# Norms in steps between products at four seams of two fused blocks, other banks for the outward products, other engines for the splits

## The chip, the cores and the metric

One core of a Trainium2 chip runs the whole program. The metric is the device time of one execution in microseconds (us); lower is better. A kernel's time is the median of its runs, and one further execution was taken by the profiler.

## What is computed

Two transformer blocks one after the other on x of 1024 tokens by 1024 features, all in float32. The first: attention over a chosen subset of keys, then a gated FFN with a short convolution (width 2816), both under adaptive norms. The second: a sliding-window attention beside a linear recurrence, then an FFN of width 4096. Cut to what the change touches:

```python
# first block
x = x + gt_m * dsa_mixer(rmsnorm(x, g_mix) * (1 + sc_m) + sh_m)
h = rmsnorm(x, g_ffn) * (1 + sc_f) + sh_f
x = rmsnorm(x + gt_f * conv_ffn(h), g_final)
# second block
u = rmsnorm(h, g_pre_mix)
mix = concat(attention(u), recurrence(u)) @ w_out
h = h + rmsnorm(mix, g_post_mix)
u = rmsnorm(h, g_pre_ffn)
f = square(relu(u @ w_ff1)) @ w_ff2
h = h + rmsnorm(f, g_post_ffn)
```

Each rmsnorm needs the sum of squares of a token over all 1024 features before any normed value of the token exists.

## The kernel before

Features lie on the 128 partitions in 8 tiles, tokens along a row in two halves (hf = 0, 1) of 512. A float32 product is made of three matmuls (`mm3`): each operand is split into a high part and a remainder (`wh` by ScalarE in `hi`, `wl` by VectorE or GpSimd in `lo`), and low by high, high by low and high by high are added in PSUM. One k-step of 128x512 is three matmuls on TensorE (PE). PSUM has eight banks; `pairs` 0 and 1 are banks 0 to 3 taken two by two, and shown as pair_70 and pair_71 in the orders and rows; banks 4 to 7 are bank_72 to bank_75. `self.psum(...)` says which banks each kind of tile takes in turn.

A norm is: squares on ScalarE, added up on VectorE or GpSimd (`square_sums`), summed over the partitions by PE against a column of ones (`token_sums`, shown as `ones,sq`), a reciprocal root of 12 operations of 128x4 on VectorE (`rstd`, rows rv, rs_t, ry), a broadcast by PE (`bcast`, shown as `ident,ry`), and a multiply per tile that reads the broadcast's bank.

PE's instructions run in the order in which the program is written (`MANUAL`). The other engines' orders are set by the framework's scheduler from its own estimate of when things are ready; each engine then runs its queue strictly in order. Buffers in SBUF are 49 equal slots (`slot`, `free`), handed out first in, first out; SyncE (SP) issues the loads and stores in order.

The four seams:
- **A.** `dsa_out` makes the output tiles of the attention and, after each half, that half's norm; `ffn_lead` then makes the first two feature tiles F0 and F1 of the FFN, half 0 before half 1, u and g each. F0 writes into pairs, F1 into banks 4 to 7. GpSimd runs `weight_sums` (adds of weights for the seven-product method, rows rt, ra, rb) and half of the splits beside it.
- **B.** `ffn1` ends with the gate of the last tiles: t is multiplied (L1358) out of a pair, and GpSimd makes s and v of a pair of tiles (L1304), which are stored. `seven_out` then runs seven products P1, P5, P2, P6, P3, P7, P4, each over 11 k-steps, whose banks `out_plan` alternates between banks 0 to 3 and 4 to 7. `make` loads and splits ahead.
- **C.** `between(hf)` is the norm after the first FFN and the one of the second block in one. Its half 1 runs over `second`, between the units of half 0 (a unit is 24 matmuls): sums after unit `UNIT_AT[0]`, broadcast after `UNIT_AT[1]`.
- **D.** `seven_lead` makes, for n = 0 to 15, a product "11" (12 matmuls) and, one n later, "12" (12 matmuls) into the same bank; between them stand the steps of `mix_norm(1)` (sums, broadcast with the combinations fa for the next stage), `mix_out(0)` and `mix_out(1)` (the sums and roots of other norms). `LEAD_AT` says after which n. `ahead` loads weights three n ahead and splits them two ahead, on GpSimd and VectorE in turn.

## Time and profile before

| | us |
|---|---|
| median of 3 runs | 2335.28 |
| lowest, highest | 2328.22, 2336.17 |
| the profiled execution, its own time | 2344.45 |
| its span, first to last instruction | 2342.7 |

| engine | busy us | share |
|---|---|---|
| PE (TensorE) | 2149.9 | 92% |
| DVE (VectorE) | 1381.5 | 59% |
| ACT (ScalarE) | 1033.8 | 44% |
| POOL (GpSimd) | 883.1 | 38% |

The mean granted clock of TensorE over the span is 0.959 of full speed. The stages lie in the span about so: attention to 592, first FFN 596 to 1098, its outward products 1105 to 1321, second block's units and attention 1321 to 1667, lead of the last FFN 1667 to 1790, the rest of it to the end. How to read it: a row of the timeline gives start, length, engine, line, operation with its output and inputs by their names, and in brackets how long the engine stood idle before and which instruction released it.

### The profile page before, as it was taken

What the parts mean: (1) busy time and instruction counts of PE and PEld (TensorE: products, weight loads), DVE (VectorE), ACT (ScalarE), POOL (GpSimd) and SP (SyncE); (2) the same over time, 40 slices, a digit from 0 to 9 for tenths busy, and PEclk for the clock granted to TensorE, in tenths of its full rate; (3) what the DMA queues carried; (4) which work ended last, traced back from release to release, by engine and by line L of the source; (5) the groups of instructions that cost most, each with busy time, mean ns of one, the idle gap of its engine ahead of it and who ended that gap; (6) DMA issues with size and microseconds to landing.
All of it is one profiled execution on the core that took longest, in us unless ns stands there. A gap on an engine that the chain in (4) does not pass through costs nothing.

```text
span 2342.7 us, 28433 instructions
## 1 busy us (share of the span) xinstructions
PE 2149.9 (92%) x10073; PEld 1785.7 (76%) x10073; DVE 1381.5 (59%) x2306; ACT 1033.8 (44%) x1623; POOL 883.1 (38%) x557
## 2 busy tenths in 40 slices
PE   5875899998799999998999899999888999999997
PEld 4664788976588888887788777788667888788886
DVE  8889686789421111122667777685673554643475
ACT  4765566643121221222443366765464443544441
POOL 6225331054366756656442422233341444201002
PEclk8977999999899999999999999999999999999999
DMA  7001131174366667686997422124255776866571
GB/s 281 1 9 52 42 99 37 46 266 165 126 202 236 240 207 236 233 275 238 323 338 279 144 69 67 55 64 154 89 211 204 261 241 221 318 195 201 191 258 54
DMA packets 165442, 405.60 MB, mean 173 GB/s; under 512 B 18441, under 2 KB 19761, under 8 KB 165298
## 3 DMA queue, kind: packets, MB, share of 16 engines
q1 hardware_dynamic: 164144, 399.58, 49.9%
q10 hardware_dynamic: 1154, 4.20, 0.5%
q8 instruction: 79, 1.29, 0.2%
q14 instruction: 65, 0.53, 0.1%
HBM read 292.28 MB, written 111.43 MB: 172 GB/s over the span
## 4 chain that ended last, share of the span: by engine, by line
PE 59%; DVE 11%; DMA 8%; POOL 4%; issue 3%; ACT 3%; SPq 0%; DVEq 0%; POOLq 0%; ACTq 0%
PE pair L208 29%; PE bank L208 27%; DVE ada L387 1%; POOL wlo L228 1%; DMA tc<-ra 1%; DMA early<-e 1%; DMA ada<-in_ada_dram 1%; POOL rt L2034 1%; DMA ra<-in_ff_dram 1%; PE bank L1134 1%; DVE sq L306 1%; DVE wl L228 1%; DMA rb<-in_ff_dram 1%; DMA st<-hs 1%; POOL rb L2034 1%
## 5 line engine op out<-in xcount | busy, mean ns | idle before, releaser
L208 PE MATMUL pair<-h,whi 128*128 128x512 f32 x1408 | 439.2, 394 | 3.2 <-DVE h L343 3.1
L228 POOL TENSOR_TENSOR wlo<-wraw,whi 128x1024 fp32r<-128x1024 f32 x98 | 245.5, 2511 | 435.1 <-ACT whi L225 310.6
L228 DVE TENSOR_TENSOR wl<-st,wh 128x1024 fp32r<-128x1024 f32 x189 | 250.3, 1341 | 207.3 <-ACT wh L225 141.0
L225 ACT ACTIVATE wh<-st 128x1024 fp32r<-128x1024 f32 x189 | 197.4, 1059 | 297.7 <-PE pair L208 67.6
L208 PEld LDWEIGHTS pair<-h,whi 128*128 128x128 f32 x1408 | 267.8, 191 | 62.2 <-DVE h L343 6.6
L208 PE MATMUL pair<-h,wlo 128*128 128x512 f32 x704 | 277.5, 396 | 28.9 <-ACT h L225 19.9
L225 ACT ACTIVATE whi<-wraw 128x1024 fp32r<-128x1024 f32 x121 | 127.1, 1056 | 313.2 <-POOL wlo L228 137.0
L343 DVE SCALAR_TENSOR_TENSOR t<-pair,vec,t 128x1023 f32<-128x1023 f32 (+1 forms) x42 | 53.8, 1282 | 261.7 <-ACT t L1350 250.0
L208 PE MATMUL pair<-wh,wl 128*128 128x512 f32 x432 | 170.4, 394 | 16.1 <-DVE t L1358 7.5
L208 PEld LDWEIGHTS pair<-h,wlo 128*128 128x128 f32 x704 | 133.8, 190 | 59.0 <-issue 23.6
L208 PE MATMUL pair<-wl,wh 128*128 128x512 f32 x432 | 169.3, 392 | 0.0
L208 PE MATMUL pair<-wh 128*128 128x512 f32 x432 | 169.1, 391 | 0.0
L208 PE MATMUL bank<-u,whi 128*128 128x512 f32 x448 | 141.7, 398 | 0.0
L2327 POOL TENSOR_TENSOR acc<-acc,grow 128x512 f32<-128x512 f32 x16 | 23.3, 1468 | 292.0 <-ACT sq L2326 292.0
L208 PE MATMUL bank<-fa,wh 128*128 128x512 f32 x416 | 130.0, 394 | 0.0
L208 PE MATMUL bank<-wh,wl 128*128 128x512 f32 x324 | 127.4, 393 | 0.0
L208 PE MATMUL bank<-wh 128*128 128x512 f32 x324 | 126.4, 390 | 0.0
L208 PE MATMUL bank<-wl,wh 128*128 128x512 f32 x324 | 126.2, 389 | 0.0
L208 PE MATMUL pair<-fa,wh 128*128 128x512 f32 x352 | 111.3, 398 | 0.0
L208 PEld LDWEIGHTS pair<-wh,wl 128*128 128x128 f32 x432 | 81.8, 189 | 36.2 <-DVE t L1358 8.0
L208 PEld LDWEIGHTS bank<-u,whi 128*128 128x128 f32 x448 | 86.6, 193 | 18.0
L208 PEld LDWEIGHTS pair<-wh 128*128 128x128 f32 x432 | 81.8, 189 | 17.2
(504 smaller groups left out, 4981.6 us busy)
## 6 DMA issues: line engine op xcount, KB each, us to landing
st<-hs SPq DMA_DIRECT2D x173, 256.0 KB, 4.2
ada<-in_ada_dram SPq DMA_DIRECT2D x48, 512.0 KB, 6.0
wraw<-in_f_in_dram SPq DMA_DIRECT2D x44, 512.0 KB, 4.1
wraw<-in_w_in_dram SPq DMA_DIRECT2D x33, 512.0 KB, 3.6
ra<-in_ff_dram SPq DMA_DIRECT2D x32, 512.0 KB, 4.5
rb<-in_ff_dram SPq DMA_DIRECT2D x32, 512.0 KB, 5.5
st<-td SPq DMA_DIRECT2D x64, 256.0 KB, 3.6
hs<-s SPq DMA_DIRECT2D x54, 256.0 KB, 3.7
```

The lines of the kernel that those rows point to most:

```text
L208: self.nc.tensor.matmul(out, w, x, start=start, stop=stop, **k)
L225: self.nc.scalar.activation(out, src, AF.Copy, **k)
L228: (eng or self.nc.vector).tensor_tensor(out, src, hi.bitcast(F32), op=ALU.subtract)
L306: (eng or nc.vector).tensor_tensor(acc, acc, sq, op=ALU.add)
L343: (eng or self.nc.vector).scalar_tensor_tensor(out, a, s, b, op0=op0, op1=op1)
L387: nc.vector.scalar_tensor_tensor(raw, raw, 1.0, self.cond, op0=ALU.mult, op1=ALU.mult, accum_out=c)
L1134: nc.tensor.transpose(ps[:, at:at + P], pr[j][:, bs(kt)], self.ident)
L2034: add = lambda o, a, b: nc.gpsimd.tensor_tensor(o, a, b, op=ALU.add)
L2327: self.nc.gpsimd.tensor_tensor(a, a, self.grow[:, hs(i)], op=ALU.mult)
```

## The change

`dsa_out` now makes the norm of half 0 alone. That of half 1 is a generator, `ffn_norm`, stepped in `ffn_lead`: squares before the first product, sums and root after u of F0, half 0, broadcast and multiply after g of F0, half 0. `ffn1` gives it banks 7 and 5.

`out_plan` takes `swap=True` for the first FFN: P1, P2, P3 and P4 go to banks 4 to 7 and P5, P6 and P7 to banks 0 to 3. The norm's banks 0 and 4 there change places.

`UNIT_AT` is (2, 3) instead of (1, 2), and `between(1)` squares tiles 4 to 7 before 0 to 3.

`LEAD_AT` now names an n and a place (0 after its "11", 1 after the "12" that follows): the steps stand at (2, 0), (2, 1), (3, 1), (6, 1), (14, 0). The first four weights of the lead are split on GpSimd, all others on VectorE. The products' banks go round as 4, 5, 6, 7, 2, 0 instead of 0, 2, 4, 5, 6, 7. The stores in `mix_out` stand before its root.

```diff
@@ -72,8 +72,9 @@
 WSTART = 4
 VLATE = 2
 MIX_AT = (1, 3, 7)
-LEAD_AT = (0, 1, 2, 12, 14)
-UNIT_AT = (1, 2)
+LEAD_AT = ((2, 0), (2, 1), (3, 1), (6, 1), (14, 0))
+LEAD_BY_POOL = 4
+UNIT_AT = (2, 3)
 SUM_BY = lambda nc: (None, nc.gpsimd)
 REST2 = 2
 UNITS2 = ((4, 5, 0, 1, 6, 7, 8, 9, 2, 3, "scan", 10, 11, 12, 13), (6, 7, 8, 9, 4, 5, "scan", 0, 1, 2, 3, 10, 11, 12, 13))
@@ -1276,21 +1277,32 @@
                     self.free(*self.oT.values())
             self.free(*self.po[hf])
             self.mod_steps(len(self.steps) - KT)
-            r = self.rstd(self.sumsq([x1[m][:, hs(hf)] for m in range(KT)]), D)
-            packs[hf] = self.norm_mod(x1, hf, r, self.gsf, 3)
+            if hf == 0:
+                r = self.rstd(self.sumsq([a[:, hs(0)] for a in x1]), D)
+                packs[0] = self.norm_mod(x1, 0, r, self.gsf, 3)
         self.hp = packs
 
+    def ffn_norm(self):
+
+        acc = self.square_sums([a[:, hs(1)] for a in self.x1])[0]
+        yield
+        r = self.rstd(self.token_sums(acc), D)
+        yield
+        self.hp[1] = self.norm_mod(self.x1, 1, r, self.gsf, 3)
+
 
     def ffn1(self):
 
         nc = self.nc
-        self.psum(main=[4, 5, 6, 7], MAIN=[0, 1], U=[0, 1], fo=[4, 5, 6, 7])
+        self.psum(main=[4, 5, 6, 7], MAIN=[0, 1], U=[0, 1], fo=[4, 5, 6, 7], ssq=[7], rb=[5])
         self.rot["G"] = self.rot["U"]
         self.ahead = (4, 2)
         st = nc.sync.dma_start
         sums = self.chain(self.weight_sums(*self.t_out1), self.weight_sums(*self.t_in2), self.weight_sums(*self.t_out2))
         lo, hi = slice(0, HF), slice(HF, S)
-        lead = self.ffn_lead()
+        norm = self.ffn_norm()
+        next(norm)
+        lead = self.ffn_lead(norm)
         t = {}
         for n, f in enumerate(FFN1):
             t[n % 2] = lead[n] if n < 2 else self.ffn_in(f)
@@ -1311,7 +1323,7 @@
             self.free(a, b, s, v)
             if n == NF1 - 3:
                 self.out_plan(NF1 // 2, self.I["f_out"], self.t_out1[1], AHEAD_OUT1,
-                              [lambda k, i=i: self.hs1[k][i] for i in (0, 3, 1, 4, 6, 5, 2)])
+                              [lambda k, i=i: self.hs1[k][i] for i in (0, 3, 1, 4, 6, 5, 2)], True)
                 self.make(0)
         self.free(*self.hp[0], *self.hp[1])
         self.ffn1_out(sums)
@@ -1323,13 +1335,15 @@
                 self.mm3(ps[:, hs(hf)], self.terms(self.weights((kind, f)), self.hp[hf]))
         return self.ffn_gate(f, pu, pg)
 
-    def ffn_lead(self):
+    def ffn_lead(self, norm):
+
 
         pairs = self.bank2("u"), self.bank2("g")
         apart = [[self.bank("fo") for _ in range(2)] for _ in range(2)]
         for hf in range(2):
             for j, kind in enumerate("ug"):
                 self.mm3(pairs[j][:, hs(hf)], self.terms(self.weights((kind, FFN1[0])), self.hp[hf]))
+                next(norm, None)
             for j, kind in enumerate("ug"):
                 self.mm3(apart[j][hf], self.terms(self.weights((kind, FFN1[1])), self.hp[hf]))
         return [self.ffn_gate(FFN1[0], *pairs), self.ffn_gate(FFN1[1], *apart)]
@@ -1398,7 +1412,7 @@
 
         def hook(name, k):
             if (name, k) in NORM1_AT:
-                self.rot.update(ssq=deque([0]), rb=deque([4]))
+                self.rot.update(ssq=deque([4]), rb=deque([0]))
                 next(norm, None)
             if (name, k) == ("P4", 6):
                 self.ahead = AHEAD2
@@ -1424,7 +1438,9 @@
             nc.vector.tensor_tensor(self.gf2, self.vall("g_final"), self.vall("g_final"), op=ALU.mult)
             self.up, self.r1 = {}, {}
         xs = [self.x1[m][:, hs(hf)] for m in range(KT)]
-        a1, a2 = self.square_sums(xs, [self.gf2[:, m:m + 1] for m in range(KT)], SUM_BY(nc)[hf])
+
+        order = [*range(4, KT), *range(4)] if hf else range(KT)
+        a1, a2 = self.square_sums([xs[m] for m in order], [self.gf2[:, m:m + 1] for m in order], SUM_BY(nc)[hf])
         yield
         ps = self.bank("ssq")
         for i, a in enumerate((a1, a2)):
@@ -1890,6 +1906,10 @@
         xs = [self.mx[hf][m // 2][:, m % 2] for m in range(KT)]
 
         sq = self.square_sums(xs)[0]
+        for m in range(4):
+            nc.sync.dma_start(self.x3[hf, m], self.mx[hf][m])
+        if hf:
+            self.free(*self.mx[0], *self.mx[1])
         yield
         r = self.rstd(self.token_sums(sq), D)
         e = self.eps4[hf] = self.const(f"eps4_{hf}", [P, 4])
@@ -1897,10 +1917,6 @@
         nc.vector.tensor_tensor(e, e, e, op=ALU.mult)
         nc.vector.reciprocal(e, e)
         nc.vector.tensor_scalar(e, e, EPS, None, op0=ALU.mult)
-        for m in range(4):
-            nc.sync.dma_start(self.x3[hf, m], self.mx[hf][m])
-        if hf:
-            self.free(*self.mx[0], *self.mx[1])
 
     def second(self):
         self.psum(main=[4, 5, 6, 7], ga=[0], gx=[2], vT=[0], ssq=[1], rb=[3])
@@ -1936,7 +1952,7 @@
 
     def second_mix(self):
 
-        self.psum(main=[4, 5, 6, 7], f1=[0, 2, 4, 5, 6, 7], ssq=[0], rb=[1, 2, 3])
+        self.psum(main=[4, 5, 6, 7], f1=[4, 5, 6, 7, 2, 0], ssq=[0], rb=[1, 2, 3])
         self.residual(0)
         norm, out = self.mix_norm(0), self.mix_out(0)
         next(norm)
@@ -1955,9 +1971,8 @@
         norm, out = self.mix_norm(1), self.mix_out(1)
         next(norm)
         steps += [norm, norm, out, out]
-        G, V = self.nc.gpsimd, self.nc.vector
         self.seven_lead(NPAIR2, lambda n: self.I["ff1"][n], self.fa, self.relu_square, self.early,
-                        dict(zip(LEAD_AT, steps)), deque([V, G]))
+                        dict(zip(LEAD_AT, steps)))
         self.ffn2_in()
         self.ffn2_out()
 
@@ -2068,7 +2083,7 @@
         self.nc.scalar.activation(out, src, AF.Relu)
         self.nc.scalar.activation(out, out, AF.Square)
 
-    def seven_lead(self, N, src, fa, put, early, at, by):
+    def seven_lead(self, N, src, fa, put, early, at):
 
         raw, w = deque(), deque()
 
@@ -2076,8 +2091,7 @@
             while len(w) + len(raw) + got[0] < min(n + 3, N):
                 raw.append(self.load("r0", src(len(w) + len(raw) + got[0])))
             while raw and len(w) + got[0] < min(n + 2, N):
-                by.rotate(1)
-                w.append(self.split_here(raw.popleft(), by[0]))
+                w.append(self.split_here(raw.popleft(), self.nc.gpsimd if len(w) + got[0] < LEAD_BY_POOL else None))
 
         got = [0]
         before = None
@@ -2088,6 +2102,7 @@
                 got[0] += 1
                 self.prod(ps, [a[:, :HF] for a in ab], fa["11"])
                 self.nc.scalar.activation(e[:, :HF], ps, AF.Copy)
+                next(at.get((n, 0), iter(())), None)
             if before:
                 m, wb, eb, pb = before
                 self.prod(pb, [a[:, HF:] for a in wb], fa["12"], True)
@@ -2095,8 +2110,7 @@
                 self.nc.sync.dma_start(early[m], eb)
                 self.free(*wb, eb)
             before = n, ab, e, ps
-            if n in at:
-                next(at[n], None)
+            next(at.get((n, 1), iter(())), None)
         self.free(*fa.pop("11"), *fa.pop("12"))
 
     def seven_in(self, N, fa, load, split, dest, mid, end, before_last):
@@ -2145,9 +2159,11 @@
         last()
         self.free(*[a for k in fa.values() for a in k])
 
-    def out_plan(self, N, right, sums, ahead, left):
+    def out_plan(self, N, right, sums, ahead, left, swap=False):
 
         X, Y = self.banks[:4], self.banks[4:]
+        if swap:
+            X, Y = Y, X
         b = lambda i, j: lambda k: right[k + N * i][:, hs(j)]
         t = lambda i: lambda k: sums[k][i]
         self.plan2 = [(n, left[i], Y if i in (1, 3, 5) else X, n in ("P2", "P7"), r) for i, (n, r) in enumerate((
```

What this does to the orders, at three places. PE at A, before, from the end of F0's u of half 0 (`h` are the normed rows, `ident,ry` is the broadcast of half 1):

```order
L208 MATMUL pair_70<-h_5535,wlo_5779 128x512
L208 MATMUL pair_70<-h_5535,whi_5778 128x512 x2
L339 MATMUL pair_71<-ident,ry_5839 128x128 x4
L208 MATMUL pair_71<-h_5500,wlo_5906 128x512
L208 MATMUL pair_71<-h_5500,whi_5905 128x512 x2
```

And in the change, two pieces, the first at the end of F0's u, the second at the end of its g:

```order
L209 MATMUL pair_70<-h_5535,whi_5778 128x512 x2
L313 MATMUL bank_75<-ones,sq_5813 128x1 x4
L209 MATMUL pair_71<-h_5500,wlo_5843 128x512
```

```order
L209 MATMUL pair_71<-h_5530,whi_5842 128x512 x2
L209 MATMUL pair_71<-h_5535,wlo_5843 128x512
L209 MATMUL pair_71<-h_5535,whi_5842 128x512 x2
L340 MATMUL bank_73<-ident,ry_5879 128x128 x4
L209 MATMUL bank_72<-h_5500,wlo_5847 128x512
```

The sums stood before F0's u and stand behind it; the broadcast stood between u and g, in the same pair as g, and stands behind g in a bank of its own.

GpSimd (POOL) at C, before: the seven adds of the squares (`sq`) with two weight splits (`wlo`) among them, all behind the splits of half 0's normed rows (`u`):

```order
L228 TENSOR_TENSOR u_1523_10592<-nt_1517_10570,u_1523_10592 128x512
L228 TENSOR_TENSOR u_1525_10600<-nt_1516_10569,u_1525_10600 128x512
L228 TENSOR_TENSOR wlo_1562_10858<-wraw_1553_10798,whi_1561_10857 128x1024
L306 TENSOR_TENSOR sq_1542_10732<-sq_1542_10732,sq_1544_10736 128x512
L306 TENSOR_TENSOR sq_1542_10732<-sq_1542_10732,sq_1545_10740 128x512
L228 TENSOR_TENSOR wlo_1582_10984<-wraw_1575_10939,whi_1581_10983 128x1024
L306 TENSOR_TENSOR sq_1542_10732<-sq_1542_10732,sq_1546_10744 128x512
L306 TENSOR_TENSOR sq_1542_10732<-sq_1542_10732,sq_1547_10748 128x512
L306 TENSOR_TENSOR sq_1542_10732<-sq_1542_10732,sq_1548_10752 128x512
L306 TENSOR_TENSOR sq_1542_10732<-sq_1542_10732,sq_1549_10756 128x512
L306 TENSOR_TENSOR sq_1542_10732<-sq_1542_10732,sq_1550_10760 128x512
```

And in the change:

```order
L307 TENSOR_TENSOR sq_1542_10732<-sq_1542_10732,sq_1544_10736 128x512
L229 TENSOR_TENSOR wlo_1538_10664<-wraw_1533_10655,whi_1537_10663 128x1024
L307 TENSOR_TENSOR sq_1542_10732<-sq_1542_10732,sq_1545_10740 128x512
L307 TENSOR_TENSOR sq_1542_10732<-sq_1542_10732,sq_1546_10744 128x512
L229 TENSOR_TENSOR wgl_1541_10728<-wgate_1539_10725,wgh_1540_10727 128x1024
L229 TENSOR_TENSOR u_1519_10576<-nt_1516_10569,u_1519_10576 128x512
L229 TENSOR_TENSOR u_1521_10584<-nt_1515_10568,u_1521_10584 128x512
L229 TENSOR_TENSOR u_1523_10592<-nt_1517_10570,u_1523_10592 128x512
L229 TENSOR_TENSOR u_1525_10600<-nt_1516_10569,u_1525_10600 128x512
L229 TENSOR_TENSOR wlo_1559_10833<-wraw_1553_10798,whi_1558_10832 128x1024
L307 TENSOR_TENSOR sq_1542_10732<-sq_1542_10732,sq_1547_10748 128x512
L307 TENSOR_TENSOR sq_1542_10732<-sq_1542_10732,sq_1548_10752 128x512
```

Three adds stand ahead of the splits of the normed rows, four behind them.

VectorE (DVE) at D, before: the combinations of `mix_norm(1)` (sb, sa, fa) and the split of the lead's sixth weight (n = 5), `wl`:

```order
L343 SCALAR_TENSOR_TENSOR mix_13468<-mix_13468,vec,pair_71 128x512 x2
L343 SCALAR_TENSOR_TENSOR sb_13704<-mix_13195,vec,sa_13703 128x512
L343 SCALAR_TENSOR_TENSOR fa_13787<-mix_13407,vec,fa_13787 128x512
L343 SCALAR_TENSOR_TENSOR sa_13703<-mix_12621,ngpf,sb_13704 128x512
L343 SCALAR_TENSOR_TENSOR fa_13790<-mix_13407,vec,fa_13790 128x512
L343 SCALAR_TENSOR_TENSOR sb_13714<-mix_12943,vec,sa_13703 128x512
L228 TENSOR_TENSOR wl_13837<-r_1963_13799,wh_13836 128x1024
L228 TENSOR_TENSOR fa_13707<-sb_13704,fa_13707 128x512
L343 SCALAR_TENSOR_TENSOR fa_13793<-mix_13468,vec,fa_13793 128x512
```

And in the change, where the splits are those of n = 5 and n = 6:

```order
L229 TENSOR_TENSOR wl_13837<-r_1927_13683,wh_13836 128x1024
L344 SCALAR_TENSOR_TENSOR sb_13739<-mix_13195,vec,sa_13738 128x512
L344 SCALAR_TENSOR_TENSOR fa_13822<-mix_13411,vec,fa_13822 128x512
L344 SCALAR_TENSOR_TENSOR sa_13738<-mix_12621,ngpf,sb_13739 128x512
L344 SCALAR_TENSOR_TENSOR fa_13825<-mix_13411,vec,fa_13825 128x512
L344 SCALAR_TENSOR_TENSOR sb_13749<-mix_12943,vec,sa_13738 128x512
L229 TENSOR_TENSOR fa_13742<-sb_13739,fa_13742 128x512
L229 TENSOR_TENSOR wl_13872<-r_1967_13834,wh_13871 128x1024
L344 SCALAR_TENSOR_TENSOR fa_13828<-mix_13472,vec,fa_13828 128x512
```

n = 5 is split before the combinations instead of among them; n = 6, which GpSimd split before, now stands among them.

## Rows read from the trace of the kernel before

**Rows 1.** The page's part 1: busy us, share of the span, instructions.

```profile
PE 2149.9 (92%) x10073; PEld 1785.7 (76%) x10073; DVE 1381.5 (59%) x2306; ACT 1033.8 (44%) x1623; POOL 883.1 (38%) x557
```

**Rows 2.** Busy time by stretches; the first line names the columns.

```profile
core 0: us, PE busy (x) PEld busy (x) DVE busy (x) ACT busy (x) POOL busy (x), PEclk, DMA share, GB/s
...
606.70:623.70 17.00, 5.61 (x16) 4.58 (x17) 13.73 (x19) 5.46 (x8) 2.93 (x2) 0.50 0.38 122
...
1337.10:1350.80 13.70, 8.90 (x29) 7.74 (x30) 7.46 (x19) 1.86 (x3) 4.51 (x4) 0.50 0.00 1
...
1675.00:1685.30 10.30, 6.97 (x20) 5.83 (x21) 8.28 (x25) 0.58 (x2) 0.00 (x0) 0.50 0.00 0
...
1712.60:1722.80 10.20, 5.47 (x13) 4.31 (x14) 10.20 (x13) 6.89 (x12) 2.38 (x1) 0.50 0.38 153
...
638.00:1098.00 460.00, 459.25 (x2024) 379.39 (x2023) 87.80 (x74) 94.46 (x89) 291.77 (x198) 1.00 0.67 225
```

**Rows 3.** Timeline of PE at A; start, us, operation, [idle before <-releaser].

```profile
591.76 0.61 PE L208 MATMUL bank<-o,whi 128*128 128x512 f32 x2
...
595.19 1.05 PE L312 MATMUL pair<-ones,sq 128*128 128x1 f32 x8 [2.81 <-DVE sq L306]
...
609.90 2.07 PE L339 MATMUL pair<-ident,ry 128*128 128x128 f32 x8 [6.09 <-DVE ry L287]
...
620.16 0.76 PE L208 MATMUL pair<-h,wlo 128*128 128x512 f32 x1 [8.19 <-DVE nt L343]
```

**Rows 4.** Timeline of DVE at A: small operations of the root, first, one between, last.

```profile
596.28 0.16 DVE L320 TENSOR_SCALAR rv<-pair 128x4 f32<-128x4 f32 x1 [1.15 <-PE pair L312]
...
601.12 1.21 DVE L286 TENSOR_TENSOR rs_t<-rs_t,rv 128x4 f32<-128x4 f32 x1
...
609.68 0.16 DVE L287 SCALAR_TENSOR_TENSOR ry<-rs_t,ry 128x4 f32<-128x4 f32 x1
```

**Rows 5.** Timeline of POOL at A, beside them: last add, last split.

```profile
606.07 1.26 POOL L2034 TENSOR_TENSOR rb<-rt,rb 128x512 f32<-128x512 f32 x1
...
607.30 2.33 POOL L228 TENSOR_TENSOR wlo<-wraw,whi 128x1024 fp32r<-128x1024 f32 x1
```

**Rows 6.** Timeline of DVE, the same operations at another norm: first and last.

```profile
1633.54 0.16 DVE L320 TENSOR_SCALAR rv<-pair 128x4 f32<-128x4 f32 x1 [3.19 <-PE pair L312]
...
1635.72 0.16 DVE L287 SCALAR_TENSOR_TENSOR ry<-rs_t,ry 128x4 f32<-128x4 f32 x1
```

**Rows 7.** Timeline of PE at B.

```profile
1105.72 0.80 PE L208 MATMUL pair<-wh,wl 128*128 128x512 f32 x1 [7.53 <-DVE t L1358]
...
1123.01 0.50 PE L208 MATMUL pair<-wh,wl 128*128 128x512 f32 x1 [1.91 <-DVE wl L228]
```

**Rows 8.** Timelines of DVE, POOL and ACT at B.

```profile
1104.46 1.21 DVE L1358 TENSOR_TENSOR t<-t,pair 128x1024 f32<-128x1024 f32 x1
...
1108.44 2.31 POOL L1304 TENSOR_TENSOR v<-t,s 128x512 f32<-128x512 f32 x1
...
1117.41 1.06 ACT L225 ACTIVATE wh<-st 128x1024 fp32r<-128x1024 f32 x1 [4.07 <-DMA hs<-s]
```

**Rows 9.** Timeline of PE at C.

```profile
1341.90 3.58 PE L1432 MATMUL pair<-ones,sq 128*128 128x1 f32 x16 [9.14 <-POOL sq L306]
```

**Rows 10.** Timeline of POOL at C: the adds of the squares.

```profile
1327.67 3.37 POOL L306 TENSOR_TENSOR sq<-sq,sq 128x512 f32<-128x512 f32 x2 [2.89 <-DVE sq L300]
...
1333.78 8.06 POOL L306 TENSOR_TENSOR sq<-sq,sq 128x512 f32<-128x512 f32 x5
```

**Rows 11.** Timeline of PE at D.

```profile
1675.63 1.87 PE L312 MATMUL pair<-ones,sq 128*128 128x1 f32 x8 [4.79 <-ACT e L2090]
...
1680.19 0.79 PE L208 MATMUL pair<-fa,wl 128*128 128x512 f32 x1 [2.70 <-DVE res L343]
...
1717.33 0.80 PE L208 MATMUL bank<-fa,wl 128*128 128x512 f32 x1 [7.70 <-DVE wl L228]
```

**Rows 12.** Timeline of DVE at D: a split.

```profile
1716.06 1.21 DVE L228 TENSOR_TENSOR wl<-r,wh 128x1024 fp32r<-128x1024 f32 x1
```

## The prediction

> **What bounds the kernel now.** I read the page first: TensorE is busy 92% of the span [rows 1], so the time is its matmuls plus the places where it stands still. The table by stretches of time comes next: through the first FFN's products it is busy 459.25 of 460.00 us in 2024 matmuls, 0.227 us each, at full clock [rows 2]. The same table shows four other stretches at a granted clock of 0.50, the lower of the two levels (1.2 instead of 2.4 GHz) [rows 2]. The timeline of PE between those points then gives the waits, all at the places that the diff touches, where one stage ends and a norm stands before the next:
> - A, before the FFN's first products: 2.81 us for the squares, 6.09 for the reciprocal root, 8.19 for the normed rows [rows 3];
> - B, before the outward product P1: 7.53 us for the last gate, then 1.91 for a split [rows 7];
> - C, in the second block's first units: 9.14 us for the squares [rows 9];
> - D, in the lead of the last FFN: 4.79, 2.70 and 7.70 us [rows 11].
>
> Together A 17.1, B 9.4, C 9.1, D 15.2. After waits of this length the products run at half clock. One product of four k-steps is 12 matmuls, 2.72 us; a pair is 5.45.
>
> **A, second half's norm among the first products.** Now PE does: last output tile, u(F0) of half 0, token sums, g(F0), broadcast, then u and g of F1 and half 1. The output tiles end at 592.4 (591.76 + 0.61 [rows 3]), so u(F0), 24 matmuls, ends at 597.8; the squares that PE waited for until 595.19 are then there, and the 2.81 is gone. g(F0) has its own bank, no longer the one whose second reader was the broadcast, so the 8.19 goes too: nt, which took from the broadcast until 620.16, is covered by F1's 10.9 us. What stays is the root. Its 12 small VectorE operations ran from 596.28 to 609.84 [rows 4], and beside them GpSimd's chain of adds and splits, which ended at 609.63 (607.30 + 2.33) [rows 5]; most of the small ones last 1.2 us, as long as one add of 1.26. Elsewhere the same 12 take 0.16 each, 2.3 from first to last [rows 6]. GpSimd's order is not changed here, so a root that starts at 598.0 runs beside the same adds. I take the end at 609.8 as before. PE then idles from g(F0)'s end, 603.2, to 609.9 and works at half clock for a while, as it does from 606.7 to 623.7 now (5.61 us busy at 0.50, so 2.8 lost [rows 2]). Before, half 1 began g(F0) and F1 after 620.16: 5.45 + 10.9 + 1.9 for half clock = 638.4. After: 610.8 + 10.9 + 2.6 = 624.3. **A: -14.** Bounds: if the root takes 2.3 us nothing waits, and half 1 begins at 592.4 + 21.8 + 1.0 = 615.2, -23; if every one of the 12 lasts 1.2 us from 598.0 and GpSimd's chain is pushed back with them, the end is 612.6 and one more add, -10.
>
> The Trainium skill, "SBUF — State Buffer", section "SBUF: two separate sides", says that VectorE and GpSimd share one port pair by an exclusive lock: who comes second waits for the whole instruction of the other, if the VectorE operation has two SBUF inputs or runs in a two-port mode. By that rule the root stays as slow as it is for as long as the adds last, and A is the 14, not the 23. The rows agree: 1.21 beside 1.26, 0.16 alone.
>
> **B, P1 on the other four banks.** P1 need not wait for the last gate's banks, so its k = 0 to 3 can begin where the wait began, 1098.2 (1105.72 - 7.53), instead of 1105.72. But its k = 4 and 5 need splits whose buffers are those of the last pair's t, s and v: the multiply that ends the last gate runs at 1104.46, GpSimd's v at 1108.44 to 1110.75, and ScalarE's part of the split for k = 5 waited for the store of s until 1117.41 [rows 8]. Nothing of this is moved by the change, and PE waits at k = 5 in the trace of before too, until 1123.01 [rows 7]. So the first 7.53 us are moved, not removed: four k-steps earlier, then idle until about 1121. **B: 0**, from +1 (half clock in a longer wait) to -3.
>
> **C, the hf = 1 sums in two parts.** Four of the eight squares move into P4. GpSimd's seven adds took 3.37 (two) and 8.06 (five) [rows 10], 1.63 each, and the last ended at 1341.84, 0.06 before PE went on. Three adds go ahead, 4.9 us of its queue, and the sums stand after three units instead of two, 5.5 us later: 10.4 against the wait of 9.14. So the wait goes, and with it the half clock from 1337.1 to 1350.8 (8.90 us busy at 0.50, 4.5 lost [rows 2]). The broadcast after the next unit gives the root 5.5 us, more than its 2.3. In P4 the added squares delay the packs of half 0 on VectorE, which I price at 1 us. **C: -12.5**, from -13.6 (all) to -8 (9.14 less what the wait keeps if the last four adds stand behind the packs).
>
> **D, steps at 2, 2, 3, 6, 14 and other split engines.** The sums that PE took at 1675.63 came after one product; in the change four products, 10.9 us, stand before them, 8.2 us more against a wait of 4.79, so it goes [rows 11]. The 2.70 is n = 1's product in the bank that the residual's broadcast held; the product now has bank 5. Both half-clock stretches go in part: 6.97 and 5.47 us busy at 0.50, 3.5 and 2.7 lost [rows 2]. The 7.70 came from a split that stood on VectorE behind the norm's own combinations (at 1716.06 [rows 12]), which in turn take what GpSimd's adds of mix and res leave ready. Those remain in the order, now with every split from n = 4 on VectorE: by walking the order I expect waits of about 2, 3.7 and 3 us at n = 5, 6 and 7, and 2 for a later load. So of 15.2 + 6.2 = 21.4, and some 2 of smaller waits, 10.7 are left. **D: -13**, from -23 (none left) to -3 (the 7.70 comes back twice, with its half clock).
>
> The half-0 norm's rows move by a few places on PE; taken as 0.
>
> **Sum.** 14 + 0 + 12.5 + 13 = 39.5 us. The profiled execution is 2344.45 by itself, 9.2 (0.4%) above the median 2335.28, so 2305.0 there and **2295.8** as a median.
>
> **Rivals.**
> 1. *Every wait goes.* A -23, B -3, C -13.6, D -23: -62.6, 2272.7. For it: the small operations cost 0.16 alone. Against: the adds beside them are not moved [rows 5].
> 2. *A is given back at B.* The FFN's end may be set not by TensorE but by the stores and loads behind GpSimd (the split that holds the last multiply, 1104.46 [rows 8]). Then B's idle time grows by A's 14: -25.5, 2309.8. Against: PE has no gap in 460 us, while GpSimd is busy 291.77 and the DMA share is 0.67 [rows 2], so both have room.
> 3. *D's waits come back* at the next splits: D -3, 2305.8. Together with 2, -15.5: 2319.8.
> 4. *Slower: VectorE becomes the bound of the lead.* It was busy 10.20 of 10.20 us from 1712.6 to 1722.8 [rows 2], with one split in that time [rows 12]. If one split in 10.2 us lasts for all eleven products n = 5 to 15, each waits 4.75 us beyond its 5.45: 52.3 us in sum, 12.8 slower than before, 2348.1. It decides if VectorE needs over 9.0 us (5.45 and a share of 39.5 / 11) for each n. Against: the combinations that fill those 10.2 us are one norm's and end; after them VectorE idles.
>
> **How the numbers follow.** Forecast 0.57; rival 1 0.10; 2 0.15; 3 0.12, with both 0.02; 4 0.04. A change under 0.5% (11.7 us, about what can be told from none) needs a gain under 11.7: the double give-back's near half and part of others, 0.07. Faster 0.89, slower 0.04. Range: from rival 1, 2272, to just short of the double give-back, 2318, which leaves out rival 4 and the tails. The forecast's own bounds, -31 to -49, lie inside.
>
> **What would show it.** A: no wait on the squares, about 6 us on ident,ry after g(F0), none on nt, half 1 near 624. B: P1 starts where the FFN ends, and a wait of 8 or more at its k = 4 or 5. C: no wait on ones,sq beyond 1 us, clock 1.00 after it. D: no wait at n = 0 and 1, several of 2 to 4 from n = 5 on. Wrong would be: a root of 2.3 us at A; P1 through k = 7 without a wait; a wait over 5 at C; over 15 us in sum at D.

## The result and the profile after

The changed kernel took 2307.45 us as the median of 4 runs (2301.88 to 2313.96) beside 2333.43 for the kernel before: a ratio of 0.9892, 95% interval 0.9859 to 0.9925. Two later timings gave 0.9872 (0.9847 to 0.9897) and 0.9875 (0.9853 to 0.9897). So it is faster by 1.1 to 1.3%, some 26 to 31 us; 39.5 had been forecast.

The page of the changed kernel, part 1 (compare [rows 1]):

```profile
PE 2147.1 (93%) x10073; PEld 1783.5 (77%) x10073; DVE 1386.2 (60%) x2310; ACT 1030.9 (45%) x1623; POOL 871.9 (38%) x553
```

The span went from 2342.7 to 2304.0. TensorE's busy time is nearly the same, 2147.1 against 2149.9: what went is waiting. Cut at the same instructions of PE in both kernels (us; two profiles of the kernel before and three of the changed one, taken in different runs):

| stretch | before | changed | mean change | forecast |
|---|---|---|---|---|
| start to the last output tile | 592.0, 590.8 | 592.0, 589.3, 595.3 | +0.8 | 0 |
| A: to half 1 of the FFN | 46.3, 46.8 | 32.3, 31.7, 31.6 | -14.7 | -14 |
| half 1 to the last product of the FFN | 457.6, 456.7 | 456.7, 456.7, 456.7 | -0.4 | 0 |
| B: to the start of P5 | 43.8, 35.8 | 36.3, 39.5, 39.1 | -1.5 | 0 |
| P5, P2, P6, P3 | 119.7, 119.7 | 119.7, 119.7, 119.7 | 0 | 0 |
| P7 | 31.7, 31.7 | 36.4, 34.1, 33.7 | +3.0 | 0 |
| P4 and the wait for the first unit | 30.6, 30.6 | 33.2, 33.3, 33.3 | +2.6 | in C |
| C: first to ninth unit | 64.4, 64.7 | 52.5, 54.1, 54.1 | -11.0 | C: -12.5 |
| ninth unit to the lead | 281.7, 276.2 | 280.1, 280.2, 280.6 | +1.3 | 0 |
| D: the lead, and two products more | 129.5, 130.3 | 118.3, 116.5, 117.3 | -12.5 | -13 |
| the rest | 535.2, 535.4 | 536.6, 534.9, 537.9 | +1.2 | 0 |

A and B came out near their forecasts. C brought 11.0 where it was looked for, but 5.6 went back in P7 and before the first unit. The stretch of D ends where PE waits for the third product of the next stage. From n = 0 to the last "12" alone it is 118.8 and 119.5 us before and 110.1, 108.2 and 108.6 after, a change of -10.2; the other 2.3 are that later wait, which the forecast did not count. The row of that wait on PE, before and in the changed kernel:

```profile
1797.29 0.79 PE L208 MATMUL pair<-fa,wl 128*128 128x512 f32 x1 [5.08 <-DVE u L2124]
```

```profile
1757.49 0.50 PE L209 MATMUL pair<-fa,wl 128*128 128x512 f32 x1 [2.66 <-DVE u L2138]
```

The first pair of profiles differs by 38.7 us, more than the medians. 7.5 of that is at B, where the first profile of before was 8 us longer than the second one. The mean changes of the table add up to 31 us.

A in the changed kernel, timeline of PE; the rows that answer to [rows 3]:

```profile
609.63 2.08 PE L340 MATMUL bank<-ident,ry 128*128 128x128 f32 x8 [5.49 <-DVE ry L288]
```

The waits of 2.81 and 8.19 are gone and the one on the root is left, 5.49 against 6.09. The root's operations on VectorE (first, one between, last) and GpSimd's last add and split beside them:

```profile
598.61 0.16 DVE L321 TENSOR_SCALAR rv<-bank 128x4 f32<-128x4 f32 x1 [4.03 <-PE bank L313]
...
600.62 1.20 DVE L286 SCALAR_TENSOR_TENSOR rs_t<-ry 128x4 f32<-128x4 f32 x1
...
609.41 0.16 DVE L288 SCALAR_TENSOR_TENSOR ry<-rs_t,ry 128x4 f32<-128x4 f32 x1
...
605.60 1.26 POOL L2049 TENSOR_TENSOR rb<-rt,rb 128x512 f32<-128x512 f32 x1
...
606.82 2.33 POOL L229 TENSOR_TENSOR wlo<-wraw,whi 128x1024 fp32r<-128x1024 f32 x1
```

Seven of the 12 take 1.11 to 1.22 us, as in [rows 4] and [rows 5], and one takes 2.26 beside the split of 2.33.

B: P1 starts where the FFN's products end, and waits at its sixth k-step (PE; against 7.53 and 1.91 in [rows 7]):

```profile
1098.97 0.50 PE L209 MATMUL bank<-wh,wl 128*128 128x512 f32 x1 [4.02 <-DVE wl L229]
```

The last gate's multiply on VectorE, and ScalarE's part of a split, which waited for a store (compare [rows 8]):

```profile
1084.93 1.21 DVE L1372 TENSOR_TENSOR t<-t,pair 128x1024 f32<-128x1024 f32 x1
...
1095.73 1.06 ACT L226 ACTIVATE wh<-st 128x1024 fp32r<-128x1024 f32 x1 [3.56 <-DMA hs<-s]
```

C: the wait of 9.14 [rows 9] is gone. Three shorter ones are new on PE: before the sums inside P7, before the first unit, and between its seventh and ninth unit:

```profile
1262.52 1.71 PE L1448 MATMUL bank<-ones,sq 128*128 128x1 f32 x13 [1.16 <-DVE sq L307]
...
1306.56 0.47 PE L209 MATMUL bank<-u,wlo 128*128 128x512 f32 x1 [2.45 <-DVE u L1404]
...
1351.01 0.72 PE L209 MATMUL pair<-xs,wgh 128*128 128x512 f32 x2 [2.56 <-DVE xs L229]
```

The wait before the first unit ends with VectorE's reading of P4's banks, which stands behind the packs of half 0:

```profile
1304.06 1.75 DVE L229 TENSOR_TENSOR u<-nt,u 128x512 fp32r<-128x512 f32 x1
1305.73 1.27 DVE L1404 TENSOR_TENSOR u<-u,bank 128x512 f32<-128x512 f32 x2
```

The second half of the sums, weighted adds on VectorE and plain adds on GpSimd:

```profile
1314.62 5.18 DVE L344 SCALAR_TENSOR_TENSOR sq<-sq,gf,sq 128x512 f32<-128x512 f32 x3
...
1312.40 6.85 POOL L307 TENSOR_TENSOR sq<-sq,sq 128x512 f32<-128x512 f32 x4
```

1.73 and 1.71 us each, side by side.

D, timeline of PE, the waits over 1 us in the lead (compare [rows 11]):

```profile
1647.91 0.50 PE L209 MATMUL bank<-fa,wl 128*128 128x512 f32 x1 [3.04 <-ACT e L2104]
...
1670.01 0.79 PE L209 MATMUL pair<-fa,wl 128*128 128x512 f32 x1 [5.45 <-DVE mix L344]
...
1715.58 0.80 PE L209 MATMUL pair<-fa,wl 128*128 128x512 f32 x1 [4.03 <-DVE wl L229]
```

ScalarE's copy of the product "11" of n = 0, which released the sums before [rows 11] and the first "12" in the change; the row of before, then that of the changed kernel:

```profile
1675.00 0.58 ACT L2090 ACTIVATE e<-pair 128x512 f32<-128x512 f32 x1
```

```profile
1647.28 1.06 ACT L2104 ACTIVATE e<-bank 128x512 f32<-128x512 f32 x2
```

VectorE's multiplies by the broadcast, the split behind them, and GpSimd's adds of mix and res:

```profile
1664.60 5.36 DVE L344 SCALAR_TENSOR_TENSOR mix<-mix,vec,pair 128x512 f32<-128x512 f32 x8 [4.12 <-PE pair L340]
...
1669.87 1.58 DVE L229 TENSOR_TENSOR wl<-r,wh 128x1024 fp32r<-128x1024 f32 x1
...
1665.42 11.81 POOL L1867 TENSOR_TENSOR mix<-mix,res 128x512 f32<-128x512 f32 x8 [20.07 <-DVE mix L344]
```

And the granted clock (PEclk, the third column from the end, as in [rows 2]) at P7's end, in units behind the ninth, and behind the wait at n = 4:

```profile
1262.50:1273.30 10.80, 10.78 (x41) 9.05 (x42) 7.07 (x21) 0.23 (x1) 0.00 (x0) 0.68 0.19 49
...
1430.80:1457.00 26.20, 23.66 (x100) 18.66 (x100) 17.07 (x40) 19.46 (x41) 6.82 (x4) 0.80 0.13 41
...
1670.00:1673.50 3.50, 3.49 (x8) 2.81 (x9) 1.57 (x2) 0.88 (x2) 3.50 (x3) 0.50 0.51 99
```

### The profile page after: what moved, and what is told of

The parts are those of the page before. It is cut to its first block, busy times and chain, and to the rows that moved or that the text cites. A ratio compares the mean times of both kernels' runs of the same rounds, so it can differ in the third digit from the quotient of the medians.

```text
span 2304.0 us, 28392 instructions
## 1 busy us (share of the span) xinstructions
PE 2147.1 (93%) x10073; PEld 1783.5 (77%) x10073; DVE 1386.2 (60%) x2310; ACT 1030.9 (45%) x1623; POOL 871.9 (38%) x553
## 5 line engine op out<-in xcount | busy, mean ns | idle before, releaser
L209 PE MATMUL pair<-wh,wl 128*128 128x512 f32 x388 | 153.7, 396 | 6.3 <-DVE acc L2304 2.6
L209 PE MATMUL pair<-wl,wh 128*128 128x512 f32 x388 | 152.7, 394 | 0.0
L209 PE MATMUL pair<-wh 128*128 128x512 f32 x388 | 152.5, 393 | 0.0
L209 PE MATMUL bank<-wh,wl 128*128 128x512 f32 x368 | 145.1, 394 | 4.0 <-DVE wl L229 4.0
L209 PE MATMUL bank<-wh 128*128 128x512 f32 x368 | 144.2, 392 | 0.0
L209 PE MATMUL bank<-wl,wh 128*128 128x512 f32 x368 | 144.0, 391 | 0.0
L209 PE MATMUL bank<-fa,wh 128*128 128x512 f32 x448 | 138.2, 390 | 0.0
L209 PE MATMUL pair<-fa,wh 128*128 128x512 f32 x320 | 102.5, 402 | 0.0
L1372 DVE TENSOR_TENSOR t<-t,pair 128x1024 f32<-128x1024 f32 x21 | 25.6, 1221 | 122.3 <-PE pair L209 119.9
L209 PEld LDWEIGHTS bank<-fa,wh 128*128 128x128 f32 x448 | 84.3, 188 | 17.5
```

The costliest lines, as they stand in the source:

```text
L209: self.nc.tensor.matmul(out, w, x, start=start, stop=stop, **k)
L1372: nc.vector.tensor_tensor(t, t, pg, op=ALU.mult)
```

## The experiments

The kernels are named by the labels of the expectations. Those with one profile and one time are read by the stretches of the table; the lead's length is there that of its row D.

**The kernel before, again**, unchanged.

> The kernel before once more, for a second profile. The profiled pair lies 38.7 us apart (2342.7 and 2304.0 of span), the medians 26 us. Theory 1: the first profile of before was long by some 10 us in places that the change does not touch; then this profile has a span near 2333 and some stage outside the four seams is shorter by several us. Theory 2: executions vary at the seams themselves, where stores and loads decide (B above all): then the stages between agree within 1 us and the end of the first FFN or the start of P5 (1139.7 in the first profile) differs by 5 us or more.

Span 2328.9. Outside the seams the stretch behind the ninth unit was 5.5 us shorter (theory 1), and B was 8.0 us shorter (theory 2): each holds in part. At B the last gate's multiply had no late load before it. Behind the ninth unit PE waits at least as long as in the first profile, but the clock did not fall. This profile is the exception: in the 13 others, before, changed and experiments, the clock over the 26 us from that wait on was 0.80. Three rows: the first of these waits on PE here, the same one in the changed kernel, and the table by stretches for the 26 us from it on here (clock 1.00; the changed kernel's 0.80 stands above):

```profile
1449.90 0.50 PE L208 MATMUL pair<-xs,wgl 128*128 128x512 f32 x1 [2.10 <-ACT xs L225]
```

```profile
1430.88 0.58 PE L209 MATMUL pair<-xs,wgl 128*128 128x512 f32 x1 [2.13 <-ACT xs L226]
```

```profile
1449.80:1476.00 26.20, 21.68 (x116) 17.28 (x117) 19.96 (x45) 20.59 (x43) 8.74 (x5) 1.00 0.12 41
```

**The changed kernel, again.**

> The changed kernel once more, timed. Both theories of the scatter: a ratio inside 0.986 to 0.9925. Theory 1: its seams come out as in the first profile of it (half 1 of the FFN at 624, P5 at 1117, lead of the last FFN from 1639 to 1757). Theory 2: P5's start lies 4 us or more elsewhere, measured from half 1's start (493.0 us in the first profile).

0.9872 (0.9847 to 0.9897), inside what was expected. From half 1 to P5 the time was 496.2 against 493.0: B scatters in the changed kernel too, by 3.2 us. The third profile gave 495.8.

**Copies on ScalarE for GpSimd's adds at A.**

```diff
-        add = lambda o, a, b: nc.gpsimd.tensor_tensor(o, a, b, op=ALU.add)
+        first = dsts is self.t_out1[1]
 ...
+            if first and i < 3:
+                add = lambda o, a, b: nc.scalar.activation(o, a, AF.Copy)
 ...
```

> The changed kernel with the adds of the first three weight sums made as copies on ScalarE instead of adds on GpSimd (this leaves those sums out, so what is multiplied by them is not the reference's). Theory lock: the root at A is slow only because GpSimd's adds run beside it: its small operations fall from 1.2 us to 0.16 except beside a weight split, the root is ready by about 602, the wait of 5.49 us before the broadcast falls under 1 us and half 1 of the FFN begins near 616 instead of 624.2. Rival: the 12 operations are slow for another reason (their own waits): 5 us or more of the wait stays and half 1 begins at 622 or later.

The root's first and last operation on VectorE:

```profile
599.95 0.17 DVE L321 TENSOR_SCALAR rv<-bank 128x4 f32<-128x4 f32 x1 [2.44 <-PE bank L313]
...
602.13 0.16 DVE L288 SCALAR_TENSOR_TENSOR ry<-rs_t,ry 128x4 f32<-128x4 f32 x1
```

0.16 us each, 2.3 from first to last; no wait before the broadcast. From F0's u to half 1 it took 23.6 us against 31.4 to 32.1. GpSimd's next split came at 605.41, after the root. So the root's slowness at A is GpSimd's work beside it, the adds above all: shown.

**The broadcast after u of F1.**

```diff
-                next(norm, None)
+                if j == 0:
+                    next(norm, None)
             for j, kind in enumerate("ug"):
                 self.mm3(apart[j][hf], ...)
+                if j == 0:
+                    next(norm, None)
```

> The changed kernel with the broadcast of half 1 after u of F1, half 0, instead of before it. If the 5.49 us are only a matter of place, u(F1) fills them: the broadcast waits under 1.5 us, no half clock follows, half 1 begins near 617 (592.2 + 43.5 halves' worth of products is 614, and the normed rows of half 1 need about 3 us after g(F1)), 7 us earlier than 624.2; ratio about 0.986. Rival: the normed rows become the wait: they need 8 us from the broadcast for the first and g(F1) covers 5.45; then half 1 starts at 620 or later. Second rival: what is won is given back at the end of the FFN (P5 at 1117 as now).

PE, the broadcast and the one wait of the normed rows:

```profile
610.77 1.05 PE L340 MATMUL bank<-ident,ry 128*128 128x128 f32 x8
...
621.16 0.74 PE L209 MATMUL pair<-h,whi 128*128 128x512 f32 x2 [0.92 <-DVE h L344]
```

The broadcast waits for nothing, half 1 begins 23.6 us after F0's u, and one late row costs 0.92. So place was the matter, and A is 7.9 us shorter. But the ratio, 0.9874 (0.9844 to 0.9904), is that of the changed kernel in the same call, 0.9872; 0.986 was expected. What scatters from run to run is as large, so these runs do not show whether all of it reaches the end.

**Without the exchange of banks.**

```diff
-                              [lambda k, i=i: self.hs1[k][i] for i in (0, 3, 1, 4, 6, 5, 2)], True)
+                              [lambda k, i=i: self.hs1[k][i] for i in (0, 3, 1, 4, 6, 5, 2)])
-                self.rot.update(ssq=deque([4]), rb=deque([0]))
+                self.rot.update(ssq=deque([0]), rb=deque([4]))
```

> The changed kernel without the exchange of banks (P1 to P4 on banks 0 to 3 again, the norm's banks back). Theory seat: the wait of 2.45 before the first unit comes from the exchange, since P4 now ends in the banks the unit writes, and VectorE empties them only behind the packs: without it P4's start to the first unit takes 30.6 us as before instead of 33.2, and the end of the FFN to P5 takes as long as with it (36 to 40 us; the kernel before: 36 to 44), so the exchange is worth nothing at B: ratio about 0.984 to 0.989. Rival (the exchange works at B): the end of the FFN to P5 is 44 us or more, ratio over 0.992. Rival to seat (the added squares delay the packs): P4's start to the first unit stays over 32.5.

0.9870 (0.9844 to 0.9895): no gain of the exchange can be told. B took 36.9 us, as with it, and P4 with the wait for the first unit 30.6 as before, so that wait belongs to the exchange. In its place the sums are late in the units, and half clock follows (PE's row, then the table by stretches):

```profile
1318.20 1.87 PE L1448 MATMUL pair<-ones,sq 128*128 128x1 f32 x8 [1.27 <-DVE sq L344]
...
1318.20:1325.00 6.80, 6.80 (x20) 5.74 (x21) 6.22 (x20) 1.08 (x3) 0.00 (x0) 0.50 0.38 127
```

P7 to ninth unit is 121.0 us without the exchange and 121.0 to 122.2 in the changed kernel.

**The exchange of banks alone** (the same two places, put into the kernel before).

> The kernel before with the exchange of banks alone. Theory seat: P4's start to the first unit grows from 30.6 to 31.5 to 33.3; the end of the FFN to P5 between 35 and 40 us, so P1's early k-steps win nothing against the second profile of before (35.8). Rival: the end of the FFN to P5 takes 33 us or less (the exchange removes the wait on the last gate), and P4's start to the first unit stays 30.6.

B took 38.8 us, inside the expected 35 to 40. P4 with the first unit stayed 30.6: the second half of theory seat missed. The exchange alone does not make that wait; it needs another part of the change as well. By VectorE's order that is the added squares, which stand before the packs; the two together, without A and D, were not tried. The stretch of the lead, unchanged here, took 133.3, 3 to 4 more than in the two profiles of before.

**C alone** (`UNIT_AT = (2, 3)` and the order of the squares, in the kernel before).

> The kernel before with the seam C alone (sums in two parts, steps after units 3 and 4). Expected of the gain: from the first unit to the ninth (u8) 64.5 us in the kernel before, 52.5 to 54.1 in the changed one. Theory seat: here the same 52 to 54, and P4's start to the first unit 30.6 to 31.2, so that 10 us or more of C's gain stay; the wait of 2.56 on xs between the seventh and ninth unit, which the kernel before does not have, is here too (u6 to u8 16.5 instead of 13.7), because the units now run without the pause in which VectorE caught up. Rival: the wait before the first unit (33.2) is C's own, from squares that delay the packs.

First to ninth unit 58.4 us, not 52 to 54: a gain of 6.1. P4 kept its 30.6. The two waits on PE:

```profile
1333.40 1.71 PE L1433 MATMUL pair<-ones,sq 128*128 128x1 f32 x8 [1.02 <-DVE sq L343]
...
1363.82 0.81 PE L208 MATMUL pair<-xs,wgh 128*128 128x512 f32 x2 [2.56 <-DVE xs L228]
```

The sums are still 1.02 late, and what they wait for is VectorE's weighted add. The wait on xs is here too, so it is C's own. The stretch of the lead, unchanged here as well, took 126.6: over four profiles the unchanged lead lies between 126.6 and 133.3, the changed one in three between 116.5 and 118.3.

**Other banks in the lead.**

```diff
-        self.psum(main=[4, 5, 6, 7], f1=[4, 5, 6, 7, 2, 0], ssq=[0], rb=[1, 2, 3])
+        self.psum(main=[4, 5, 6, 7], f1=[4, 5, 6, 7, 0, 2], ssq=[0], rb=[1, 2, 3])
```

> The changed kernel with the lead's banks in the order 4, 5, 6, 7, 0, 2 instead of 4, 5, 6, 7, 2, 0. Theory pair: the 5.45 us at n = 4 is a wait for the readers of the broadcast in bank 3, because banks 2 and 3 are one tile and n = 4 writes bank 2; with bank 0 it goes (under 0.5 us at n = 4). Within it, theory chain: the splits of n = 5 and 6, which stand on VectorE behind the norm's multiplies and combinations, take over, and the lead's whole length (n = 0 to the next stage, 116.5 to 118.3 us) shrinks by 2 us at most. Rival free: the wait goes and nothing takes its place: 109 to 111 us. Rival to pair: the wait stays at 4 us or more.

The wait at n = 4 is gone: theory pair holds. Three others stand in its place, at n = 5, 6 and 11 (PE):

```profile
1673.35 0.50 PE L209 MATMUL pair<-fa,wl 128*128 128x512 f32 x1 [1.56 <-DVE wl L229]
...
1682.78 0.79 PE L209 MATMUL bank<-fa,wl 128*128 128x512 f32 x1 [3.67 <-DVE wl L229]
...
1720.85 0.79 PE L209 MATMUL pair<-fa,wl 128*128 128x512 f32 x1 [7.54 <-DVE wl L229]
```

The lead took 122.3 us, 4 to 6 longer than in the changed kernel. Theory chain foresaw the first two, 5.23 in sum against the 5.45 that went; the growth is at n = 11, 7.54 against 4.03 in the changed kernel, which it did not foresee. In both, a split just ahead of that one on VectorE waited until a stored result had given its buffer back (1.44 here, 2.22 in the changed kernel); that this is the cause was not tried.

**C's plain adds on VectorE too.**

```diff
-SUM_BY = lambda nc: (None, nc.gpsimd)
+SUM_BY = lambda nc: (None, None)
```

> The changed kernel with the plain adds of C's squares on VectorE too, none on GpSimd. In the changed kernel VectorE's last three weighted adds took 1.73 us each beside GpSimd's last four adds of 1.71, in step. Theory lock at C: without GpSimd's adds the weighted ones fall to 0.75 and a plain add costs 0.68, so a pair costs 1.43 instead of 1.73, the sums are ready 1 to 2 us sooner (relative to the first unit) and the units are no later: first to ninth unit 51 to 54 us. Rival (VectorE's own load is the limit, not what runs beside it): the weighted adds stay over 1.2 us, and the wait on ones,sq comes back, first to ninth unit over 56.

A weighted add on VectorE, and the wait before the first unit on PE (2.45 in the changed kernel):

```profile
1314.61 0.74 DVE L344 SCALAR_TENSOR_TENSOR sq<-sq,gf,sq 128x512 f32<-128x512 f32 x1
...
1306.98 0.47 PE L209 MATMUL bank<-u,wlo 128*128 128x512 f32 x1 [1.08 <-DVE u L1404]
```

The weighted adds fell to 0.74 where no GpSimd work ran, so at C too they were slow by what ran beside them. The sums were not ready sooner, though: 14.0 us after the first unit began instead of 13.2, since VectorE now does both kinds. First to ninth unit 54.1: neither better nor worse. The shorter wait before the first unit is not shown to come from the edit: it was 3.05 in the later run that has the same adds.

**Six of the lead's splits on GpSimd** (`LEAD_BY_POOL = 6`).

> The changed kernel with the first six weights of the lead split on GpSimd instead of four (n = 4 and 5 move off VectorE, one of them among the adds of mix and res). Theory chain (the lead is as long as the norm's multiplies, adds and combinations with the splits that stand among them): 2.4 us more on GpSimd before its adds are through, one split of 1.2 less on VectorE; the lead stays between 115 and 121 us. Rival (VectorE's splits are what the lead waits for): 112 us or less.

The lead took 119.3 us, inside what theory chain gave. PE's waits have moved again, from n = 11, which now waits 0.42, to 2.51 at n = 7:

```profile
1671.34 0.76 PE L209 MATMUL pair<-fa,wl 128*128 128x512 f32 x1 [5.54 <-DVE mix L344]
...
1693.52 0.50 PE L209 MATMUL bank<-fa,wl 128*128 128x512 f32 x1 [2.51 <-DVE wl L229]
```

**Later broadcast and C's adds on VectorE, beside the changed kernel itself.**

> The changed kernel with the broadcast of half 1 after u of F1 (as in the run before) and C's plain adds on VectorE, timed beside the changed kernel itself. If the 8 us that the later broadcast saved between the output tiles and half 1 reach the end: 6 to 10 us below the changed kernel, ratio 0.983 to 0.985. Rival: given back where stores, loads and the clock decide (the end of the FFN, the lead): within 3 us of it, as the first timing of the later broadcast gave.

> The changed kernel once more, beside the run above: ratio between 0.986 and 0.990, last output tile to half 1 31.5 to 32.5 us.

Five rounds: 2302.89 us, 0.9859 (0.9838 to 0.9881), beside 2305.19, 0.9875 (0.9853 to 0.9897), for the changed kernel. The intervals overlap; 2.3 us is no gain that these runs can tell, and the 6 to 10 expected did not come in the medians. A was 23.8 us long in it, against 31.6 in the changed kernel of the same call; half 1 to the last product was 1.3 longer and B 0.6. The two profiles' spans differ by 6.8, so where the rest of the 7.8 goes stays open.

## Why the prediction was right or wrong

**The whole.** 2295.8 was forecast and 2307.45 measured, inside the range of 2272 to 2318 and faster as said. The gain was 26 us, two thirds of the 39.5. In the first pair of profiles it is 38.7, which looks like the forecast and is not: 7.5 of that is B, where nothing was forecast, from the scatter of single profiles, and it hides the 7.3 that were lost in P7 and before the first unit. The table's means, 31, fall short of the sum by 8: C by 7 and the lead by 3, while the rest nearly cancels.

**A, right in size and reason.** Half 1 was to begin at 624.3 and began at 624.2. The step taken, that the root would stay slow beside GpSimd's adds, decided it, and the run without the first adds shows that: the upper bound of 23 us was the price with a root of 2.3 us, and A then takes 23.6 us from F0's u where the sum of that bound had 22.8. The Trainium skill, "SBUF — State Buffer", section "SBUF: two separate sides", says that the engine that comes second at the shared port waits for the whole instruction of the other, and the trace agrees: 1.20 us beside adds of 1.26, 2.26 beside a split of 2.33, 0.16 without.

**B, right.** 0 was forecast; the mean of the profiles is -1.5 and each kernel scatters by 3 us or more. The wait moved to the sixth k-step, as argued, and the kernel without the exchange has the same ratio as the one with it. But the sign that was named, 8 us or more there, did not come: it is 4.02 here and at most 7.36 in the ten profiles with the exchange. What was missed is that B is no fixed time: before, 35.8 and 43.8. The sum of the forecast was taken from the profile with the longer one.

**C, the mechanism right, the term mis-sized: -12.5 forecast, -5.4 measured** from P7's start to the ninth unit (126.9 to 121.5 as means), -6.1 with C alone. Of the 13.6 us of wait and half clock between the first and ninth unit, 11.0 were won net. Three steps failed.
- *"Three adds go ahead ... 10.4 against the wait of 9.14. So the wait goes."* In the changed kernel it went, but the reckoning was made with GpSimd's adds alone. VectorE's weighted adds of the same squares end last; in C alone they still hold the sums by 1.02 us. The trace of before shows it already: they ended at 1342.40, 0.56 after GpSimd's last add:

```profile
1337.51 4.89 DVE L343 SCALAR_TENSOR_TENSOR sq<-sq,gf,sq 128x512 f32<-128x512 f32 x3
```

- *"The added squares delay the packs ... 1 us."* With the exchange of banks it is 2.6: PE waits 2.45 before the first unit, since P4 now ends in the banks that the unit writes, and VectorE empties them behind the packs. The exchange alone and C alone have no such wait.
- What was not in the sum: units that no longer pause outrun VectorE. The new wait on xs is 2.56 in the changed kernel and in C alone. By VectorE's order, the rows normed for half 1 come one unit later and meet the convolution xc and xs of the next units; this was read, not tried.

The sums in P7 are those of half 0's norm, whose moved rows were "taken as 0". P7 took 33.1 to 37.2 us instead of 31.7 in six of the nine profiles that have the exchange and the new sums together, and in none of the five others. In the six, VectorE's last add ends just before the sums begin: PE waits 0.45 to 1.95 us in five of them and 0.03 in the sixth. In five the clock falls behind the sums (0.68 over 10.8 us in the first profile). Why VectorE is late there in some runs only was not settled.

**D, near in size, partly by luck, its inside only in part.** -13 was forecast; the stretch gave -12.5, but 2.3 of that are the later wait, and the lead itself gave -10.2. Its waits are 13.4 us in sum, where 10.7 were forecast. The 2.70 went, and the 4.79 only in part. Before, the sums were released not by their squares but by ScalarE's copy of the product of n = 0, which ended at 1675.58. In the change that copy ends at 1647.86, 8.7 us after the lead begins, and the first "12", which writes the same bank, waits 3.04 for it; so four products ahead of the sums did not cover it. The 2.70 was not "the bank that the residual's broadcast held", though: banks 2 and 3 are two halves of one tile, and a product in bank 2 waits for readers of bank 3. The same wait came back at n = 4 (5.45), where none was forecast; the run with other banks shows it. The waits forecast at n = 5 to 7 (2, 3.7, 3) stayed small (0.40 and 0.48 at n = 7 and 8) because the 5.45 had given VectorE the time: when it was taken away, 1.56 and 3.67 appeared at n = 5 and 6. The wait at n = 11 was forecast as 2 and was 4.03. Which of D's parts (places, engines of the splits, banks, earlier stores) won how much was not tried one by one.

**The rivals.** None decided. Rival 2, A given back at B, is refuted by the table: B is not longer. Rival 3 is refuted by the lead's 10.2. Rival 4, the lead bound by VectorE, holds as a mechanism in the small: with the wait at n = 4 removed, the splits behind the norm's work held PE for nearly as long at n = 5 and 6.

## What to carry to other kernels

A step that must end before the next product is priced by the last of all its chains, on every engine that has a part in it; here the plain adds were reckoned and the weighted ones beside them ended later. A stall that is removed also took time in which another engine caught up, so ask what that engine does in the next two or three units. And before a gain is read from two profiles, take the profile of the unchanged kernel twice: stretches that wait on stores and loads differed by 8 us here.

## What was not expected of the hardware

- The same waits did and did not lower TensorE's clock. Behind the ninth unit two waits, of 2.09 to 2.13 and 0.87 to 0.96 us, stand 1.5 us apart in every profile. In one, the second of the kernel before, the granted clock stayed at 1.00; in the 13 others it was 0.80 over the 26 us from there on. That is worth 4 to 5 us of a run.
- The wait before the narrow sums does not decide whether the clock falls behind them. In P7 the fall came after a wait of 1.16 us (P7 4.7 us longer) and after one of 0.03 (1.9 longer, clock 0.81 over 9.0 us), and it did not come after one of 1.09 (1.4 longer, clock 1.00). The two last, by stretches from the sums on, in the changed kernel timed last and in the run beside it with the later broadcast:

```profile
1266.80:1275.80 9.00, 8.97 (x41) 7.55 (x41) 6.85 (x20) 0.01 (x1) 0.00 (x0) 0.81 0.18 58
```

```profile
1261.70:1269.10 7.40, 7.39 (x41) 6.42 (x42) 6.85 (x20) 0.04 (x1) 0.00 (x0) 1.00 0.23 71
```

- Operations on 128x4 elements are not free beside GpSimd: 12 of them took 11.0 us, from 598.6 to 609.6, beside its adds and a split, and 2.3 us when the adds were copies on ScalarE and the split came later.
